# Where the context tokens stand in the loads and in the modulation of a block of gated linear attention

## The chip, the cores and the metric

The kernel runs on one core of a Trainium2 chip. The metric is the time of one execution on the device in microseconds (us). Three runs of the kernel before give a median of 1012.62 us (1012.34 to 1014.2).

The names of the engines: PE is the matrix engine (PEld its weight loads), DVE the vector engine, ACT the scalar engine, POOL the general one; SP issues most of the DMAs and computes nothing. An instruction of an engine runs when all those ahead of it on that engine have started and what it waits for is there, so one that waits holds up what stands behind it.

## What is computed

One layer of a diffusion backbone over 512 latent tokens and 256 context tokens of 1024 features, in 32-bit floats. Cut to what the change touches:

```
mod_lat = jnp.split(jax.nn.silu(c) @ w_ada + b_ada, 6, axis=-1)
mod_ctx = jnp.split(jax.nn.silu(c_ctx)[None, :] @ w_ada + b_ada, 6, axis=-1)
h_lat = modulate(rmsnorm(x, g_mix), shift, scale)      # 512 tokens
h_ctx = modulate(rmsnorm(ctx, g_mix), shift_c, scale_c)  # 256 tokens
z = h @ w_in          # q, k, v, g, dd (decay, rank 16), conv and gate columns
zd = dd @ w_dec_up + b_dec     # up-projection of the decay, 16 -> 512, two directions
log_a = log_sigmoid(zd) / 16
```

Behind that come the attention scans (the context's state is where the latent scan starts), a short convolution, the gates, an output projection, a SwiGLU layer and a last norm. They are the same before and after.

## The kernel before

Products of 32-bit precision are made of three passes: each operand is split into a high part (ACT makes it, a copy or an activation with rounding) and a low part (DVE subtracts it), and PE sums high x high, high x low and low x high. A split is thus one ACT and one DVE instruction, and PE waits for both.

The start of the kernel, some 60 us, makes the first head's q, k, v and decay columns of the latent tokens. The latent tokens (`xt`, four tiles of 128 x 1024) are loaded, normed (`normed`: ACT squares and a root, DVE a reciprocal and a product) and turned by PE into features on partitions (`turn`, the transposes `xtp`, copied out to `xsT` by ACT and DVE). Then the features are gone through in four **parts** of 256. For part p:

- `ada_load(p)` loads eight 256 KB pieces of w_ada (`wa`), `w0_load(p)` 256 rows of the needed columns of w_in in four DMAs (`r_w`, 128x2x256, 128x2x32 and twice 128x2x128 floats, 557 KB in all).
- `ada_rows(p)` multiplies `wa` on PE (`ada`), DVE copies the bank (`adar`), PE turns it to columns (`adac` in `mod_cols`), DVE makes shift and scale (`modT`, `gs`).
- `modulate(2p)` and `modulate(2p + 1)` make `h`, the modulated latent features, high part on ACT, two DVE instructions for the low one.
- `w0_split(p)` splits `r_w` (`h_w` on ACT, `l_w` on DVE), and `gather_v` and `gather_kq` add the products of k = 2p and 2p + 1 into the banks of v, k and q (`v`, `kl`, `q` on PE).

The loop over k from 0 to 7 runs one part ahead: at k = 1, 3 and 5 it splits and modulates part 1, 2 and 3. After its last part it norms the two context tiles (line 541), turns them at k = 6 (line 549) and modulates all their eight feature tiles (line 551, `mod_ctx`: `xcT` to `hc`, one ACT and two DVE instructions each). `head0_gather` then multiplies the context features (`vc`, `kc`), and ends with the transposes `ddt` of the decay's rank-16 columns, which `v_done` has put into `st`.

What sets the order: from line 481 on, the instructions of PE, ACT and DVE keep the order in which the code writes them (`keep_in_program_order`). The loads on SP don't: a planner puts a load that waits for nothing ahead of one that waits for a buffer. SP also has eight completion counters that its DMAs take in turn, so that a DMA is issued when the one eight before it has landed. Two kinds of loads wait for a buffer here: `r_w` has three buffers for four parts, so part 3's waits for the split of part 0; the context tokens take buffers of the tag `raw` that part 0's `wa` held, so they wait for PE's `ada` of part 0.

The up-projection of the decay, `wraw`, is loaded in eight copies of 16 rows by POOL at the start (line 321) and split by five DVE instructions in `wdu_split` (line 514), behind the modulation of part 0.

Of the kernel before, what the change touches and what calls it, by code (L numbers as in the profile page):

```python
# [18 lines left out]
KT = D // P  # L19
T = 512  # L20
TC = 256
NT = T // P
NC_ = TC // P
# [23 lines left out]
def hybrid_block(ctx: ExitStack, tc: tile.TileContext, x, c, ctxt, c_ctx, w_ada, b_ada, g_mix, w_in,  # L47
                 w_dec_up, b_dec, g_head, w_gla_out, w_conv, w_conv_out, w_mix_out, g_ffn,
                 w_ffn_in, w_ffn_out, g_final, out):
    nc = tc.nc  # L50
# [14 lines left out]
    def u2(name, dt=F32, shape=(P, 512)):  # L65
        return up.tile(list(shape), dt, tag="u2", name=name, bufs=NU)
# [8 lines left out]
    def uh(name, dt=F32, shape=(P, 512)):  # L75
        return up.tile(list(shape), dt, tag="uh", name=name, bufs=8)
# [29 lines left out]
    def f32(ap):  # L106
        return ap.bitcast(F32)
# [45 lines left out]
    def mm3(o, a, b, start, stop):  # L153
        mm(o, a[0], b[0], start=start, stop=False)
        mm(o, a[0], b[1], start=False, stop=False)
        mm(o, a[1], b[0], start=False, stop=stop)

    def rstd_of(ss, n, width, name):

        r = sm.tile([P, n], F32, tag=f"rs{n}", name=f"rs_{name}")  # L160
        act_.activation(r, ss, AF.Sqrt, bias=eps, scale=1.0 / width)
        dve.reciprocal(r, r)
        return r
# [4 lines left out]
    def token_load(i):  # L168
        if i < NT:
            xt = hp.tile([P, D], F32, tag="xt", name=f"xt{i}", bufs=4)  # L170
            nc.sync.dma_start(xt, x[i * P:(i + 1) * P, :])
        else:
            xt = wp.tile([P, D], F32, tag="raw", name=f"xt{i}", bufs=4)
            nc.sync.dma_start(xt, ctxt[(i - NT) * P:(i - NT + 1) * P, :])
        return xt
# [12 lines left out]
    def small_vectors(vs):  # L188
        for r0, src in vs:
            n = src.shape[1] // P  # L190
            for d in range(src.shape[0]):
                nc.sync.dma_start(vrow[r0 + d * n:r0 + (d + 1) * n, :P], src[d:d + 1, :].rearrange("o (r f) -> (o r) f", f=P))
# [52 lines left out]
    def normed(i, xt):  # L245
        junk = u2(f"junk{i}", BF16, (P, D))
        ss = sm.tile([P, 1], F32, tag="ss", name=f"ss{i}")
        act_.activation(junk, xt, AF.Square, accum_out=ss)
        dve.tensor_scalar_mul(xt, xt, rstd_of(ss, 1, D, f"x{i}"))
# [11 lines left out]
    def ada_load(p_):  # L261

        us = []
        src = w_ada[:, :2 * D].rearrange("(k p) (s f) -> p k s f", p=P, s=2)[:, :, :, p_ * 256:(p_ + 1) * 256]
        if p_ < 2:
            for k in range(0, KT, 2):
                if p_ == 0:
                    t = wp.tile([P, 2, 2, 256], F32, tag="raw", name=f"wa{p_}{k}", bufs=4)
                else:
                    t = hp.tile([P, 2, 2, 256], F32, tag="wa", name=f"wa{p_}{k}", bufs=4)  # L270
                for i in range(2):
                    nc.sync.dma_start(t[:, i], src[:, k + i])
                us += [t[:, i].rearrange("p s f -> p (s f)") for i in range(2)]
        else:
            for k in range(KT):
                t = (uh if p_ == 2 else uo)(f"wa{p_}{k}", F32, (P, 2, 256))
                nc.sync.dma_start(t, src[:, k])
                us.append(t.rearrange("p s f -> p (s f)"))
        return us

    def ada_rows(p_, us):

        rows = gbank(f"ada{p_}")
        for k in range(KT):
            g_ = 32 * (k % 4)
            mm(rows[g_:g_ + 32, :], cw[:, k, :], us[k], start=k < 4, stop=k >= KT - 4)
        rsb = u2(f"adar{p_}")
        dve.tensor_copy(rsb, rows)
        return rsb
# [5 lines left out]
    def mod_split(src, f, j, hi, lo):  # L295
        g_, sh = gs[:, f, j:j + 1], modT[:, f, 0, j:j + 1]
        act_.activation(hi, src, AF.Identity, scale=g_, bias=sh)
        dve.tensor_scalar(src, src, g_, sh, ALU.mult, ALU.add)
        dve.tensor_sub(lo, src, f32(hi))
# [13 lines left out]
    def modulate(f):  # L313
        mod_split(xsT[:, f, :], f, 0, *h[f])

    def wdu_load():
        wraw = u2("wraw")
        whi_ = u2("wdhi", F32R)
        for d in range(2):
            for r in range(4):  # L320
                nc.gpsimd.dma_start(wraw[d * 64 + r * 16:d * 64 + r * 16 + 16, :], w_dec_up[0, d])
        return wraw, whi_

    def wdu_split(wraw, whi_):
        dve.tensor_copy(whi_, wraw)
        for d in range(2):
            a = d * 64
            dve.tensor_copy(wdu[a:a + 32, :], f32(whi_)[a:a + 32, :])
            dve.tensor_sub(wdu[a + 32:a + 64, :], wraw[a + 32:a + 64, :], f32(whi_)[a + 32:a + 64, :])
# [19 lines left out]
    def run(steps):  # L349
        for _ in steps:  # L350
            pass
# [85 lines left out]
    def w0_load(p_):  # L437

        r = hp.tile([P, 2, NW + 256], F32, tag="wr", name=f"r_w0{p_}", bufs=3)
        for d0, c0, n in ((0, CV, HV), (HV, CD, 32), (NW, CK, P), (NW + P, CQ, P)):  # L440
            nc.sync.dma_start(r[:, :, d0:d0 + n], w_in[p_ * 256:(p_ + 1) * 256, c0:c0 + n].rearrange("(a p) b -> p a b", p=P))
        return r

    def w0_at(k, a, e):
        return tuple(w_[:, k % 2, a:e] for w_ in w0[k // 2])
# [12 lines left out]
    def gather(o, c0, src, k, n=T):  # L458
        mm3(o[:, :n], w0_at(k, c0, c0 + P), tuple(w_[:, :n] for w_ in src[k]), k == 0, k == KT - 1)
# [7 lines left out]

    vo = [bank(f"v0_{NC_}")]

    wdu_ = wdu_load()  # L470
    was, wrs = [], []
    for p_ in range(4):
        if p_:
            wrs.append(w0_load(p_))
        was.append(ada_load(p_))
        if p_ == 0:
            wrs.append(w0_load(p_))
    small_vectors(((R_GH, g_head), (R_BD, b_dec[0]), (R_WC, w_conv[0])))
    xcs = [token_load(NT + i) for i in range(NC_)]
    lat = (xsT[:, :4, :], xsT[:, 4:, :])  # L480
    pinned[0] = True
    normed(0, xts[0])
# [12 lines left out]
    def w0_split(p_):  # L495
        w0.append(split_raw(wrs[p_], f"w0{p_}"))

    def mod_lo(f):
        g_, sh = gs[:, f, 0:1], modT[:, f, 0, 0:1]
        src = xsT[:, f, :]  # L500
        dve.tensor_scalar(src, src, g_, sh, ALU.mult, ALU.add)
        yield
        dve.tensor_sub(h[f][1], src, f32(h[f][0]))


    w0.append(tuple(wp.tile([P, 2, NW + 256], F32R, tag=t, name=f"{t}_w00", bufs=4) for t in ("whi", "wlo")))
    act_.copy(w0[0][0], wrs[0])
    act_.activation(h[0][0], xsT[:, 0, :], AF.Identity, scale=gs[:, 0, 0:1], bias=modT[:, 0, 0, 0:1])
    lo = mod_lo(0)
    next(lo)  # L510
    dve.tensor_sub(w0[0][1], wrs[0], f32(w0[0][0]))
    run(lo)
    modulate(1)
    wdu_split(*wdu_)
    vo += [(bank if i < 3 else gbank)(f"v0_{NC_ + i}") for i in range(1, NT)]
    ko, qo = gbank("kl0"), gbank("q0")

    def mod_ctx(f):
        t = uh(f"hc{f}", F32R, (P, 2, TC))
        mod_split(xcT[f // 4][:, f % 4, :], f, 1, t[:, 0, :], t[:, 1, :])  # L520
        hc.append((t[:, 0, :], t[:, 1, :]))
# [5 lines left out]
    for k in range(KT):  # L527
        p_ = k // 2 + 1
        more = k % 2 == 1 and p_ < 4
        if more:  # L530
            w0_split(p_)
            gather_v(vo[:2], h, k)
            rsb = ada_rows(p_, was[p_])
            gather_kq(k - 1)
            mod_cols(p_, rsb)
            modulate(2 * p_)
            modulate(2 * p_ + 1)
            gather_v(vo[2:], h, k, base=2)
            if p_ == 3:
                for i in range(NC_):  # L540
                    normed(NT + i, xcs[i])
        else:
            gather_v(vo, h, k, passes=k == 0)
        if k % 2 or k >= 6:
            gather_kq(k)
        if k == 6:
            xcT = [wp.tile([P, 4, TC], F32, tag="raw", name=f"xcT{i}", bufs=4) for i in range(2)]
            for i in range(NC_):
                turn(NT + i, xcs[i], xcT, i)
            for f in range(KT):  # L550
                mod_ctx(f)
    hp.release()
    gp = tc.alloc_tile_pool(name="gp", bufs=1)
# [10 lines left out]
    def head0_gather():  # L564
        for k in range(KT + 2):
            if k < KT:
                gather_v(vc, hc, k)
            if k >= 2:
                gather(kc, NW, hc, k - 2, TC)
            if k == KT - 1:  # L570
                ddt(NC_, NC_ + NT)
                vps2 = gbank("vps2")
                tr(vps2[:, :R_N], vrow[:R_N, :P], ident[:R_N, :R_N])
                dve.tensor_copy(vec[:, 64:], vps2[:, 64:R_N])
# [370 lines left out]
    for pr in range(KT // 2):  # L945
# [24 lines left out]
        for j in range(2):  # L970
# [3 lines left out]
            hi, lo = ux(f"cuh{pr}{j}", F32R), ux(f"cul{pr}{j}", F32R)  # L974
# [20 lines left out]
    for i, t in enumerate(og):  # L995
        mk = uv if i < 3 else ux
        hi, lo = mk(f"ogh{i}", F32R), mk(f"ogl{i}", F32R)
# [3 lines left out]
    for pr in range(KT // 2):  # L1001
        ada_tick()
        sl_ = Slab(w_gla_out, pr * 256, 256, f"go{pr}")
        for j in range(2):
            i = 2 * pr + j
# [4 lines left out]
            hi, lo = ux(f"meh{i}", F32R), ux(f"mel{i}", F32R)  # L1010
# [119 lines left out]
    for pr in range(FT // 2):  # L1130
# [16 lines left out]
        for j in range(2):  # L1147
# [4 lines left out]
            hi, lo = mk(f"ah{pr}{j}", F32R), mk(f"al{pr}{j}", F32R)  # L1152
# [8 lines left out]
    for ch in range(2):  # L1161
# [9 lines left out]
        for t in range(NT):  # L1171
# [8 lines left out]
            else:  # L1180
# [4 lines left out]
                r = rstd_of(ss, 1, D, f"fin{t}")  # L1185
# [32 lines left out]
```

## Time and profile before

| | before |
|---|---|
| median of three runs | 1012.62 us |
| the profiled execution, as timed | 1013.98 us |
| its span, from first to last instruction | 1012.3 us |
| PE busy | 989.9 us (98%) |
| DVE busy | 545.7 us (54%) |
| ACT busy | 382.0 us (38%) |
| POOL busy | 6.4 us (1%) |
| data moved | 117.16 MB, mean 116 GB/s |

The start by stretches of 10 us (busy time of PE and DVE, the clock granted to PE as a share of full speed, what the DMAs moved):

| stretch, us | PE | DVE | clock | GB/s |
|---|---|---|---|---|
| 20 to 30 | 8.82 | 8.26 | 1.00 | 337 |
| 30 to 40 | 9.94 | 4.81 | 1.00 | 338 |
| 40 to 50 | 9.92 | 4.74 | 1.00 | 173 |
| 50 to 60 | 9.68 | 7.81 | 1.00 | 82 |
| 60 to 70 | 9.26 | 7.31 | 1.00 | 132 |
| 70 to 80 | 8.02 | 7.54 | 0.86 | 105 |
| 80 to 90 | 10.00 | 5.13 | 0.97 | 107 |

Busy time is read beside what the engine waited for: PE can be busy all the time and still be paced by its own order, and an engine that idles costs nothing unless another waits for it. All times below are from the start of the span of the profiled execution.

### The profile page before, as it was taken

Reading aid. Unit: us, or ns where it says so; the run is one execution under the profiler, and the core shown is the slowest. Engines: PE = TensorE matmul, PEld = TensorE weight load, DVE = VectorE, ACT = ScalarE, POOL = GpSimd, SP = SyncE. Lnnn points to the kernel's source line nnn. Section 1 sums busy time; section 2 is a strip of 40 time slices with the busy share of each in tenths; the row PEclk is TensorE's granted clock in tenths of the full one; section 3 lists DMA queues with packets and bytes.
Section 4 is the critical chain, followed back from the end, with each engine's and each line's share of the span. In section 5 each row is a group of like instructions: output and inputs, shape, how many; then the busy total and the mean of one; then the engine's idle time right before and its main releaser. Section 6 shows DMA issues by size and latency. Waiting matters only on the chain.

```text
span 1012.3 us, 12874 instructions
## 1 busy us (share of the span) xinstructions
PE 989.9 (98%) x5217; PEld 826.3 (82%) x5221; DVE 545.7 (54%) x845; ACT 382.0 (38%) x602; POOL 6.4 (1%) x18
## 2 busy tenths in 40 slices
PE   5989999999999999999999999999999999999997
PEld 3778888888788888888888888988888888888886
DVE  6577876866646677767443345643423333423424
ACT  5257464649345222224222224633322323311313
POOL 2000000000000000000000000000000000000000
PEclk9999999999999999999999999999999999999999
DMA  9841212021427776666533222242332332331302
GB/s 296 263 118 49 52 54 63 23 63 43 123 88 205 208 203 185 172 209 210 149 101 104 84 84 84 84 125 84 104 104 84 104 104 83 101 127 64 125 21 84
DMA packets 109760, 117.16 MB, mean 116 GB/s; under 512 B 5523, under 2 KB 97797, under 8 KB 109701
## 3 DMA queue, kind: packets, MB, share of 16 engines
q1 hardware_dynamic: 109444, 116.07, 38.0%
q8 instruction: 41, 0.67, 0.3%
q0 software_dynamic: 256, 0.26, 0.1%
q14 instruction: 19, 0.15, 0.1%
HBM read 114.22 MB, written 2.10 MB: 115 GB/s over the span
## 4 chain that ended last, share of the span: by engine, by line
PE 91%; DVE 4%; ACT 3%; issue 1%; DMA 1%; SPq 0%; ACTq 0%; DVEq 0%
PE f L148 24%; PE fo L148 11%; PE yc L148 4%; PE yg L148 4%; PE gb L148 4%; PE cb L148 4%; PE cc L148 4%; PE ch L148 4%; PE ga L148 4%; PE g L148 4%; PE v L148 4%; PE mx L148 3%; PE kl L148 2%; PE o L148 2%; PE q L148 2%; PE F L148 2%
## 5 line engine op out<-in xcount | busy, mean ns | idle before, releaser
L148 PE MATMUL f<-h,h_fa 128*128 128x512 f32 (+1 forms) x384 | 111.0, 372 | 0.2 <-DVE h L102 0.2
L148 PE MATMUL f<-h,h_fb 128*128 128x512 f32 (+1 forms) x384 | 110.2, 372 | 0.0
L148 PEld LDWEIGHTS f<-h,h_fa 128*128 128x128 f32 x384 | 70.2, 188 | 13.2 <-DVE h L102 0.8
L148 PEld LDWEIGHTS f<-h,h_fb 128*128 128x128 f32 x384 | 70.0, 188 | 12.4
L148 PE MATMUL f<-h,l_fb 128*128 128x512 f32 (+1 forms) x192 | 71.3, 371 | 0.0
L148 PE MATMUL f<-h,l_fa 128*128 128x512 f32 (+1 forms) x192 | 71.3, 371 | 0.0
L102 DVE TENSOR_TENSOR l_fa<-r_fa,h_fa 128x1024 fp32r<-128x1024 f32 x22 | 26.9, 1225 | 74.6 <-ACT h_fa L102 74.6
L102 DVE TENSOR_TENSOR l_fo<-r_fo,h_fo 128x1024 fp32r<-128x1024 f32 x22 | 26.9, 1224 | 68.7 <-ACT h_fo L102 68.7
L148 PE MATMUL fo<-h_fo,ah 128*128 128x512 f32 x154 | 60.5, 393 | 0.0
L148 PE MATMUL fo<-l_fo,ah 128*128 128x512 f32 x154 | 60.5, 393 | 0.0
L148 PE MATMUL fo<-h_fo,al 128*128 128x512 f32 x154 | 60.4, 392 | 0.0
L935 DVE SCALAR_TENSOR_TENSOR acc<-r_wa,c,acc 128x256 f32<-128x256 f32 x112 | 54.1, 483 | 9.1 <-DMA r_wa<-in_w_ada_dram 6.4
L102 ACT CAST h_fo<-r_fo 128x1024 fp32r<-128x1024 f32 x22 | 23.1, 1050 | 71.0 <-PE fo L148 27.4
L148 PEld LDWEIGHTS f<-h,l_fb 128*128 128x128 f32 x192 | 36.2, 188 | 6.3
L148 PEld LDWEIGHTS f<-h,l_fa 128*128 128x128 f32 x192 | 36.1, 188 | 6.3
L148 PE MATMUL g<-h,h_g 128*128 128x512 f32 x128 | 41.0, 402 | 0.0
L148 PE MATMUL gb<-h,h_gb 128*128 128x512 f32 x128 | 40.0, 394 | 0.0
L148 PE MATMUL cb<-h,h_cb 128*128 128x512 f32 x128 | 39.7, 391 | 0.0
L148 PE MATMUL ch<-h,h_ch 128*128 128x512 f32 x128 | 39.6, 390 | 0.0
L148 PE MATMUL cc<-h,h_cc 128*128 128x512 f32 x128 | 39.6, 390 | 0.0
L148 PE MATMUL ga<-h,h_ga 128*128 128x512 f32 x128 | 39.4, 390 | 0.0
L1150 DVE TENSOR_TENSOR sil<-sil,f 128x512 f32<-128x512 f32 x22 | 15.1, 687 | 39.7 <-PE f L148 39.7
(320 smaller groups left out, 2281.4 us busy)
## 6 DMA issues: line engine op xcount, KB each, us to landing
r_wa<-in_w_ada_dram SPq DMA_DIRECT2D x32, 512.0 KB
r_fa<-in_w_ffn_in_dram SPq DMA_DIRECT2D x22, 512.0 KB
r_fb<-in_w_ffn_in_dram SPq DMA_DIRECT2D x22, 512.0 KB
r_fo<-in_w_ffn_out_dram SPq DMA_DIRECT2D x22, 512.0 KB
wa<-in_w_ada_dram SPq DMA_DIRECT2D x32, 256.0 KB
r_g<-in_w_in_dram SPq DMA_DIRECT2D x8, 512.0 KB
r_gb<-in_w_in_dram SPq DMA_DIRECT2D x8, 512.0 KB
r_cc<-in_w_in_dram SPq DMA_DIRECT2D x8, 512.0 KB
```

Source lines behind the costliest of these rows:

```text
L102: return lambda *a, **k: pin(getattr(self.engine, op)(*a, **k))
L148: pe_pin(nc.tensor.matmul(*a, **k))
L935: nc.vector.scalar_tensor_tensor(acc, w_[:, k, :], ck, acc, ALU.mult, ALU.add)
L1150: nc.vector.tensor_mul(sil, sil, obs[2 + j])
```

## The change

Three things are moved, and one instruction pair is turned around. (1) In the code, the loads of the two context tiles stand behind `ada_load(1)`, ahead of part 2's loads, and no longer at the end. They are normed at k = 1, turned at k = 2, and modulated behind the latent features of the same part: feature tiles 0 to 3 at k = 3, 4 and 5 at k = 5, 6 and 7 at k = 6. (2) `wraw` is loaded on SP, behind the small vectors, instead of on POOL at the start, and split in `head0_gather` at k = 1. (3) In part 0 the low part of the weights (`wlo`) comes ahead of the features' product on DVE.

```diff
 def wdu_load():
...
-                nc.gpsimd.dma_start(wraw[d * 64 + r * 16:d * 64 + r * 16 + 16, :], w_dec_up[0, d])
+                nc.sync.dma_start(wraw[d * 64 + r * 16:d * 64 + r * 16 + 16, :], w_dec_up[0, d])
...
-    wdu_ = wdu_load()
     was, wrs = [], []
     for p_ in range(4):
...
         if p_ == 0:
             wrs.append(w0_load(p_))
+        if p_ == 1:
+            xcs = [token_load(NT + i) for i in range(NC_)]
     small_vectors(((R_GH, g_head), (R_BD, b_dec[0]), (R_WC, w_conv[0])))
-    xcs = [token_load(NT + i) for i in range(NC_)]
+    wdu_ = wdu_load()
...
     dve.tensor_scalar(src, src, g_, sh, ALU.mult, ALU.add)
-        yield
         dve.tensor_sub(h[f][1], src, f32(h[f][0]))
...
-    lo = mod_lo(0)
-    next(lo)
     dve.tensor_sub(w0[0][1], wrs[0], f32(w0[0][0]))
-    run(lo)
+    mod_lo(0)
     modulate(1)
-    wdu_split(*wdu_)
...
             gather_v(vo[2:], h, k, base=2)
-            if p_ == 3:
-                for i in range(NC_):
-                    normed(NT + i, xcs[i])
+            if p_ > 1:
+                for f in range(2 * p_ - 4 if p_ == 2 else 2 * p_ - 2, 2 * p_):
+                    mod_ctx(f)
...
-        if k == 6:
+        if k == 1:
+            for i in range(NC_):
+                normed(NT + i, xcs[i])
+        if k == 2:
             xcT = [wp.tile([P, 4, TC], F32, tag="raw", name=f"xcT{i}", bufs=4) for i in range(2)]
             for i in range(NC_):
                 turn(NT + i, xcs[i], xcT, i)
-            for f in range(KT):
+        if k == 6:
+            for f in (6, 7):
                 mod_ctx(f)
...
             if k >= 2:
                 gather(kc, NW, hc, k - 2, TC)
+            if k == 1:
+                wdu_split(*wdu_)
```

What this makes of the order on the engines. First SP before, at the end of the weights of part 2 (`wa_212` is its last piece, `r_w_214` the w_in rows of part 3, `wa_219` the first piece of part 3's w_ada):

```order
L277 DMA wa_210<-in_w_ada_dram 128x2x256
L277 DMA wa_212<-in_w_ada_dram 128x2x256
L441 DMA r_w_214<-in_w_in_dram 128x2x256
L441 DMA r_w_214<-in_w_in_dram 128x2x32
L441 DMA r_w_214<-in_w_in_dram 128x2x128 x2
L277 DMA wa_219<-in_w_ada_dram 128x2x256
```

and SP before at the end of all these loads (`wa_233` is the last piece of w_ada, `vrow` the small vectors, `xt_241` and `xt_243` the context tokens, `r_g` the first weights of the next stage):

```order
L277 DMA wa_233<-in_w_ada_dram 128x2x256
L192 DMA vrow<-in_g_head_dram 2x128
L192 DMA vrow<-in_b_dec_dram 4x128 x2
L192 DMA vrow<-in_w_conv_dram 8x128 x3
L174 DMA xt_241<-in_ctx_dram 128x1024
L174 DMA xt_243<-in_ctx_dram 128x1024
L117 DMA r_g_0_711<-in_w_in_dram 128x4x256
L117 DMA r_g_1_713<-in_w_in_dram 128x4x256
```

The same place on SP now (`wa_227` is the last piece of w_ada, `xt_183` and `xt_185` are the context tokens, `r_w_208` the w_in rows of part 3):

```order
L277 DMA wa_227<-in_w_ada_dram 128x2x256
L192 DMA vrow<-in_g_head_dram 2x128
L192 DMA vrow<-in_b_dec_dram 4x128 x2
L192 DMA vrow<-in_w_conv_dram 8x128 x3
L321 DMA wraw<-in_w_dec_up_dram 16x512 x8
L174 DMA xt_183<-in_ctx_dram 128x1024
L174 DMA xt_185<-in_ctx_dram 128x1024
L441 DMA r_w_208<-in_w_in_dram 128x2x256
L441 DMA r_w_208<-in_w_in_dram 128x2x32
L441 DMA r_w_208<-in_w_in_dram 128x2x128 x2
L117 DMA r_g_0_706<-in_w_in_dram 128x4x256
```

The context tokens stand where they stood, behind all sixteen pieces of w_ada of parts 2 and 3; `wraw` stands ahead of them, and part 3's w_in rows have gone behind them.

ACT before, from the modulation of part 1 on (`h_140` holds the features of parts 0 and 1, `h_141` those of parts 2 and 3; `h_w_448` and `h_w_512` are the weights of parts 2 and 3; `junk`, `ss` and `rs_x` belong to the context tokens' norm):

```order
L102 ACTIVATE h_140<-xsT,modT,gs 128x512 x2
L102 CAST h_w_448<-r_w_193 128x1088
L102 ACTIVATE h_141<-xsT,modT,gs 128x512 x2
L102 CAST h_w_512<-r_w_214 128x1088
L102 ACTIVATE h_141<-xsT,modT,gs 128x512 x2
L102 ACTIVATE junk_558,ss_559<-xt_241 128x1024
L102 ACTIVATE rs_x_561<-ss_559,eps 128x1
```

and ACT now from the same place (`h_w_483` and `h_w_563` are the weights of parts 2 and 3):

```order
L102 ACTIVATE h_140<-xsT,modT,gs 128x512 x2
L102 ACTIVATE junk_431,ss_432<-xt_183 128x1024
L102 ACTIVATE rs_x_434<-ss_432,eps 128x1
L102 ACTIVATE junk_438,ss_439<-xt_185 128x1024
L102 ACTIVATE rs_x_441<-ss_439,eps 128x1
L102 COPY xcT_457<-xtp_0_459 128x4x128
L102 COPY xcT_457<-xtp_0_471 128x4x128
L102 CAST h_w_483<-r_w_187 128x1088
L102 ACTIVATE h_141<-xsT,modT,gs 128x512 x2
```

The norm of the context tokens and the copies of their transposes stand ahead of everything of parts 2 and 3. On DVE it is the same, and on PE the sixteen transposes stand between the products of k = 2 and of k = 3; otherwise PE's order is as before.

## Rows read from the trace of the kernel before

**Rows 1.** Page, part 1: engine, busy us (share of the span), instructions

```profile
PE 989.9 (98%) x5217; PEld 826.3 (82%) x5221; DVE 545.7 (54%) x845; ACT 382.0 (38%) x602; POOL 6.4 (1%) x18
```

**Rows 2.** Timeline of SP's DMA issues, 30 to 46 us: start, us, instruction, count

```profile
30.60 2.53 SPq L441 DMA_DIRECT2D r_w<-in_w_in_dram  x4
33.53 5.01 SPq L277 DMA_DIRECT2D wa<-in_w_ada_dram  x8
38.59 0.32 SPq L192 DMA_DIRECT2D vrow<-in_g_head_dram  x1
...
40.67 1.79 SPq L192 DMA_DIRECT2D vrow<-in_w_conv_dram  x3
42.91 1.06 SPq L174 DMA_DIRECT2D xt<-in_ctx_dram  x2
```

**Rows 3.** Waits of SP, 38 to 46 us: us in total, times, longest

```profile
SPq L192 <- DMA wa<-in_w_ada_dram: 2.1, 5, 0.5
SPq L174 <- DMA wa<-in_w_ada_dram: 0.7, 2, 0.4
```

**Rows 4.** Windows: stretch, PE, PEld, DVE, ACT, POOL busy, clock, DMA share, GB/s

```profile
32.00:34.00 2.00, 1.94 (x12) 1.57 (x11) 1.93 (x4) 1.45 (x2) 0.00 (x0) 1.00 1.10 348
...
46.00:48.00 2.00, 2.00 (x14) 1.24 (x7) 0.69 (x1) 0.00 (x0) 0.00 (x0) 1.00 0.46 180
48.00:50.00 2.00, 2.00 (x17) 1.95 (x16) 0.33 (x2) 0.61 (x1) 0.00 (x0) 1.00 0.01 2
```

**Rows 5.** Timeline of PE: start, us, instruction, count, [idle before <- releaser]

```profile
34.41 0.43 PE L148 MATMUL v<-h_w,h 128*128 128x288 f32 x2
...
35.43 1.92 PE L148 MATMUL ada<-wa,cw 128*32 128x512 f32 x16
...
54.38 1.03 PE L151 MATMUL xtp<-ident,xt 128*128 128x128 f32 x8
...
56.61 0.38 PE L148 MATMUL v<-h_w,h 128*128 128x288 f32 x1
```

**Rows 6.** Chain of waits, 0 to 160 us: start, us, what

```profile
1.59 3.72 DMA xt<-in_x_dram
5.33 1.16 ACT junk L102 x2
```

**Rows 7.** Timeline of all engines, 0 to 14 us

```profile
7.91 3.68 PE L151 MATMUL xtp<-ident,xt 128*128 128x128 f32 x16 [4.97 <-DVE xt L102]
```

**Rows 8.** Timeline of DVE, 14 to 92 us

```profile
24.77 0.42 DVE L102 CAST wdhi<-wraw 128x512 fp32r<-128x512 f32 x1
...
27.50 1.29 DVE L102 TENSOR_TENSOR l_w<-r_w,h_w 128x1088 fp32r<-128x1088 f32 x1
...
43.39 1.28 DVE L102 TENSOR_TENSOR l_w<-r_w,h_w 128x1088 fp32r<-128x1088 f32 x1
46.72 0.69 DVE L102 COPY adar<-ada 128x512 f32<-128x512 f32 x1 [2.05 <-PE ada L148]
...
57.60 0.41 DVE L102 TENSOR_SCALAR xcT<-xcT,gs,modT 128x256 f32<-128x256 f32 x1
...
63.55 0.43 DVE L102 TENSOR_TENSOR hc<-xcT,hc 128x256 fp32r<-128x256 f32 x1
```

**Rows 9.** Timeline of PE, 14 to 92 us

```profile
48.00 0.95 PE L148 MATMUL adac<-sel,adar 128*128 128x2 f32 x8
...
69.26 0.30 PE L151 MATMUL ddt<-ident,st 128*128 128x128 f32 x1 [0.61 <-ACT st L102]
...
74.84 0.30 PE L151 MATMUL ddt<-ident,st 128*128 128x128 f32 x1 [0.92 <-ACT st L102]
75.66 0.62 PE L148 MATMUL z<-ddT,wdu 64*128 64x256 f32 x4 [0.52 <-DVE ddT L102]
```

**Rows 10.** Windows, the same columns, where the clock fell and rose

```profile
77.00:78.00 1.00, 1.00 (x4) 0.78 (x3) 0.90 (x3) 1.00 (x4) 0.00 (x0) 0.56 0.03 8
...
80.00:81.00 1.00, 1.00 (x5) 0.82 (x4) 0.27 (x1) 0.99 (x2) 0.00 (x0) 0.73 0.00 0
```

## The prediction

> **What bounds the kernel now.** The page first: PE is busy for 98% of the span [rows 1], so a change at the start pays or costs only by what it does to PE's time there. Then I read SP's issues in order of time [rows 2]. From 30 to 43 us they come in the order in which the code names them: part 3's w_in rows, part 3's eight pieces of w_ada, the small vectors, and last, at 42.91 us, the two context tokens. What paces them is not SP: each of the small vectors and of the tokens waits for a piece of w_ada to land [rows 3], eight issues back. The windows say why: while the weights come the DMAs are full, at 1.10 of their share and 348 GB/s, and after 48 us, with the tokens in, they are empty [rows 4]. This costs nothing today, since PE wants the tokens only at 54.38 us [rows 5], and between 34 and 54 us it goes from product to product without a gap worth naming.
>
> The change asks for the tokens at another time. On PE their sixteen transposes now stand between the products of k = 2 and those of k = 3. Before, that border is the second product of the row at 34.41 us, at about 34.55 us [rows 5]. So what matters is when the tokens land. In the code their load has moved ahead of part 2; on SP it has not. There it still follows the last piece of w_ada, and eight copies of `wraw` have come between. **PE will ask for the tokens at 34.5 us, and they will land at about 48.** ACT, DVE and PE keep their written order, and on all three everything of parts 2 and 3 stands behind the tokens' norm or transposes, so that nothing can run meanwhile.
>
> **When the tokens land.** (a) A small vector's issue takes 0.32 us; with the step to the next I count 0.36 for an issue that waits for nothing. Before, the second token is thus issued at 42.91 + 1.06 - 0.36 = 43.6 us, and it waits for the last piece of w_ada, which landed then [rows 2, 3]. (b) Part 3's w_in rows leave the stretch ahead of it: 557 KB at 348 GB/s are 1.6 us [rows 4]. (c) `wraw` no longer shares the DMAs at the start: 262 KB, 0.75 us; between nothing (if it slipped into gaps) and 0.75 I take the whole, since the DMAs are full. The last piece lands at 43.6 - 1.6 - 0.75 = 41.25 us. (d) By the rule of eight, the second copy of `wraw` waits for that piece, and then seven copies go ahead of the first token. If nothing holds them they cost an issue each, 0.36 us, 2.5 in all. Bounds: 0.27 each (three vectors' issues take 1.79 us with two waits in it; the least that the issues can be is about that), 1.9 us; or 0.74 each, the distance of the vectors now [rows 2], 5.2 us. I take 2.5, since what is eight back is small or landed by then. The first token is issued at 43.75 us, the second at 44.1. (e) From issue to landing the first latent token took 3.72 us [rows 6]. The second context token was issued at 43.6 and its data had ended by 48.0, when the window falls from 180 to 2 GB/s [rows 4]: 4.4 us to the last data, somewhat more to the landing; I take 4.7, between 4.4 and 5.2 (3.72, and 1.5 for the first token's 524 KB at 348 GB/s). The second token lands at 48.8 us, the first about a microsecond ahead of it.
>
> The Trainium skill ("DMA: Bandwidth & Descriptors", "Issuing engines are not separate DMA queues") says that starting DMAs on several engines saves only the issuing engine's time, which it calls usually small. By that rule moving `wraw` from POOL to SP would cost next to nothing, and the sum below would come to 1026.5 instead of 1029. I go by the issues' rows, because here eight issues stand in one queue ahead of what PE waits for.
>
> **From the landing to PE.** At the start of the kernel a latent token goes from the first square on ACT, at 5.33 us, to PE's first transpose at 7.91 us: 2.58 us for square, root, reciprocal and product [rows 6, 7]. The same for the second context token: 48.8 + 2.58 = 51.4 us. Then its eight transposes. At full clock eight take 1.03 us [rows 5]; at the start, after 4.97 us without work, sixteen took 3.68 us, 1.84 for eight [rows 7]. The half clock is granted later too: 0.56 from 77 to 78 us and 0.73 from 80 to 81, half speed from 77.1 to 80.5, after PE stood still three times within 69 to 76 us [rows 9, 10]. With some 15 us without work I take the half clock: 53.2 us, where at full clock it would be 52.4. PE resumes the products of k = 3 at 53.2 instead of 34.55 us: **18.65 us late**.
>
> **What is given back and what is added.** The transposes' old place falls away, from 54.38 to 56.61 us: -2.2 [rows 5]. A rest of half clock behind the transposes: between 0 and 1.7 (half of those 3.4 us); I take 0.4, since the gap between the two tokens' transposes counts as well. DVE: a feature tile of the context takes 0.79 us (eight from 57.60 to 63.98 [rows 8]). Four of them, 3.2 us, now stand ahead of part 3's split, which ran from 43.39 to 44.68; it would end at 47.8 and `adar` at 48.5 in old time, where PE took up `adac` at 48.00 to 48.2 [rows 8, 9]: PE waits 0.4 more. Part 3's w_in rows follow the tokens by some 2 us and are wanted 10 us after PE's resuming; they cost nothing. On ACT the same four tiles hide in its idle time.
>
> Behind k = 7 the gain that the change can have: DVE is no longer at the context's features until 63.98 us, so `v_done` and the latent `ddt` come in time, and PE's wait of 0.61 us goes [rows 9]: -0.6. The five instructions of `wdu_split`, 2.7 us (24.77 to 27.50 [rows 8]), fill most of what DVE gains there, but end before `ddt`'s copy. The waits of 0.92 and 0.52 us hang on DVE's splits behind that copy, whose distance is unchanged; I leave them, with the clock's fall at 77 us that follows. If they went too, with the clock: another -3.1. The pair that is turned around in part 0, `wdu_split`'s going from there, and the earlier loads can make PE come to the border by up to a microsecond or two sooner than 34.55. That is worth nothing: PE waits for the tokens anyway, and is late by the time at which it resumes.
>
> **Sum:** 18.65 - 2.2 + 0.4 + 0.4 - 0.6 = 16.65 us. On the profiled execution's 1013.98 us that is 1030.6; it stands 1.36 us above the median, and against the median of 1012.62 the forecast is 1029.3 us, rounded 1029.
>
> Ends: least, 1.9 us for the seven copies, 4.4 us for the landing, transposes at full clock and all the gains behind (-3.7): the second token is issued at 43.5, lands at 47.9, and PE resumes at 51.5, 16.95 late; 16.95 - 2.2 - 3.7 = +11, 1023.7. Most, no gain from `wraw`'s leaving the start (42.0), 0.74 us for each issue (the second token at 47.9), 5.2 us to land, half clock and its rest of 1.7: 53.1, resuming at 57.5, 22.95 late; 22.95 - 2.2 + 1.7 + 0.4 = +22.85, 1035.5.
>
> **The rivals.** *The tokens are there in time*, as the code reads: the loads run as written, or the DMAs serve the tokens ahead of what was issued before. The point from which it decides: both landed by 34.55 - 2.58 = 32.0 us. Then PE never waits for them. The megabyte pushes parts 2 and 3 back by 3 us, less 0.75 for `wraw`; the last piece of w_ada lands at 45.9, when PE's `ada` of part 3 is under way. What is left is +0.4 and between -0.6 and -3.7: 1009.3 to 1012.4 us. For it speaks only the source text. Against it: before, the trace's issues follow the planned order row by row [rows 2], and the 16 pieces of w_ada stand ahead in it now. 5%, three of them for faster by over 0.2% (about what a measurement of this kernel can tell from no change), two for within it.
>
> *The wait is much shorter*: SP gets through the pieces of w_ada faster without the w_in rows and POOL's copies, so that the tokens land at 38 to 46 us. That asks for over 350 GB/s where 348 is the most that these rows show. 1016 to 1023.5 us, 3%.
>
> *The wait is partly won back behind it*, since the weights of parts 2 and 3 lie ready when PE resumes. But PE had no gaps there to close: its busy time is full in the windows from 46 to 50 us [rows 4]. At most the waits counted above; this is the lower end of the forecast, no case of its own.
>
> *The tokens come later still*, if the eight copies go one landing after another: eight times 2 us or more. Over 1036 us, 3%.
>
> **How the numbers follow.** The forecast has 89%, with 1023.7 to 1035.5 us. The range 1023.5 to 1035.5 leaves out the rivals, 11%, and little of the forecast's own. Slower by over 0.2%: 0.95; within: 0.02; faster: 0.03.
>
> **What would show it.** Right: SP's issue of the context tokens at 43 to 46 us, behind all of w_ada; ACT idle from about 32.5 to 47 us until a DMA of ctx; on PE one gap from about 34 us to 50, released by DVE's `xt`, and a clock of 0.50 for some microseconds after it; PE's `xtp` of the context at 50 to 53; no wait at the latent `ddt`. Wrong: the tokens issued before 30 us; PE busy through 35 to 50 us; or a gap of that size with the time back by 160 us.

## The result, and the profile after

| | before | after |
|---|---|---|
| median | 1012.57 us (4 runs, 1012.34 to 1014.2) | 1029.91 us (4 runs, 1029.37 to 1031.88) |
| profiled execution, as timed | 1013.98 us | 1030.05 us |
| its span | 1012.3 us | 1028.3 us |
| PE busy | 989.9 us (98%) | 990.2 us (96%) |

The kernel became slower: 1.0171 times the time of before, 95% interval 1.0154 to 1.0189. PE's busy time is the same, so the 16 us of span are time in which PE stands. The runs of before fall into two groups, about 1012.5 and 1014.1 us, so that medians of before shift by some 1.1 us between the comparisons below and the ratios within one comparison are the safer numbers.

SP's issues after, in order of time (start, us, instruction, count), which answer to [rows 2]:

```profile
22.83 11.82 SPq L277 DMA_DIRECT2D wa<-in_w_ada_dram  x16
...
37.29 1.83 SPq L192 DMA_DIRECT2D vrow<-in_w_conv_dram  x3
39.47 3.78 SPq L321 DMA_DIRECT2D wraw<-in_w_dec_up_dram  x8
43.37 0.83 SPq L174 DMA_DIRECT2D xt<-in_ctx_dram  x2
44.29 2.03 SPq L441 DMA_DIRECT2D r_w<-in_w_in_dram  x4
```

The two context tokens go out at 43.37 us, behind all of w_ada and behind the eight copies of `wraw`; part 3's w_in rows follow them. The chain of waits after (start, us, what) tells what set that time, and what hung on it:

```profile
34.28 5.88 DMA wa<-in_w_ada_dram
...
40.17 0.32 SPq L321
...
42.84 0.42 SPq L321
...
43.37 3.89 DMA xt<-in_ctx_dram
...
47.34 1.16 ACT junk L102 x2
...
49.35 0.77 DVE xt L102
...
50.25 3.84 PE xtp L151 x16
```

Seven of the eight copies stand between 40.17 us, when the last piece of w_ada had landed, and 43.37 us: 3.2 us, 0.46 us each. PE's timeline after (start, us, instruction, count, idle before and its releaser) shows what PE did meanwhile; the second half answers to [rows 9]:

```profile
32.43 0.29 PE L148 MATMUL v<-h_w,h 128*128 128x288 f32 x1
50.25 3.84 PE L151 MATMUL xtp<-ident,xt 128*128 128x128 f32 x16 [17.52 <-DVE xt L102]
53.74 0.59 PE L148 MATMUL v<-h_w,h 128*128 128x288 f32 x1
...
59.76 0.38 PE L148 MATMUL v<-h_w,h 128*128 128x288 f32 x1
...
68.64 1.05 PE L148 MATMUL adac<-sel,adar 128*128 128x2 f32 x8 [0.30 <-DVE adar L102]
69.55 0.38 PE L148 MATMUL v<-h_w,h 128*128 128x288 f32 x1
...
86.60 0.60 PE L151 MATMUL ddt<-ident,st 128*128 128x128 f32 x4
...
87.86 0.63 PE L148 MATMUL g<-h,h_g 128*128 128x512 f32 x2
89.34 0.50 PE L148 MATMUL g<-h,l_g 128*128 128x512 f32 x1 [0.85 <-DVE l_g L102]
...
92.60 0.30 PE L151 MATMUL ddt<-ident,st 128*128 128x128 f32 x1 [0.92 <-ACT st L102]
93.42 0.62 PE L148 MATMUL z<-ddT,wdu 64*128 64x256 f32 x4 [0.52 <-DVE ddT L102]
...
102.97 0.28 PE L148 MATMUL v<-h_v,hc 128*128 128x256 f32 x1
```

One gap of 17.52 us, between the last product of k = 2 and the context's transposes. Windows of the same stretch (stretch; PE, PEld, DVE, ACT, POOL busy; granted clock, DMA share, GB/s), beside [rows 4]:

```profile
34.00:36.00 2.00, 0.00 (x0) 0.00 (x0) 0.00 (x0) 0.00 (x0) 0.00 (x0) 0.83 1.10 349
...
38.00:40.00 2.00, 0.00 (x0) 0.00 (x0) 0.00 (x0) 0.00 (x0) 0.00 (x0) 0.50 0.17 51
40.00:44.00 4.00, 0.00 (x0) 0.00 (x0) 0.00 (x0) 0.00 (x0) 0.00 (x0) 0.50 0.25 61
...
50.00:55.00 5.00, 4.75 (x21) 4.31 (x22) 2.59 (x6) 2.35 (x4) 0.00 (x0) 0.50 0.32 77
55.00:56.00 1.00, 1.00 (x7) 0.38 (x9) 1.00 (x1) 0.00 (x0) 0.00 (x0) 0.60 0.82 202
56.00:57.00 1.00, 1.00 (x16) 0.24 (x8) 0.07 (x1) 0.00 (x0) 0.00 (x0) 1.00 0.73 230
```

From 40 to 44 us, while SP hands out `wraw`, nothing computes and the DMAs are a quarter busy, at 61 GB/s: that stretch is bound by the issues of one queue, not by the memory. The DMAs are nearly idle even before it, at 0.17 of their share from 38 to 40 us, while SP's issues still wait one by one for the last pieces of w_ada to land, until 40.16 us; why these land so long after the data have thinned out is not shown. The clock is at its lower level (0.50, 1.2 of 2.4 GHz) until 55 us and some of the microsecond behind, so the transposes and the first products run at half speed.

### The profile page after: what moved, and what is told of

Same layout as the page of the kernel before. It is cut to its first block, busy times and chain, and to the rows that moved or that the text cites. A ratio compares the mean times of both kernels' runs of the same rounds, so it can differ in the third digit from the quotient of the medians.

```text
span 1028.3 us, 12873 instructions
## 1 busy us (share of the span) xinstructions
PE 990.2 (96%) x5221; PEld 827.2 (80%) x5221; DVE 546.2 (53%) x845; ACT 382.2 (37%) x602; POOL 2.4 (0%) x10
## 4 chain that ended last, share of the span: by engine, by line
PE 90%; DMA 3%; DVE 2%; ACT 2%; SPq 1%; issue 1%; ACTq 0%; DVEq 0%
PE f L148 23%; PE fo L148 10%; PE v L148 5%; PE yc L148 4%; PE yg L148 4%; PE gb L148 4%; PE cb L148 4%; PE ch L148 4%; PE cc L148 4%; PE ga L148 4%; PE g L148 4%; PE mx L148 3%; PE o L148 2%; PE kl L148 2%; PE q L148 2%; PE F L148 2%
## 5 line engine op out<-in xcount | busy, mean ns | idle before, releaser
L938 DVE SCALAR_TENSOR_TENSOR acc<-r_wa,c,acc 128x256 f32<-128x256 f32 x112 | 54.1, 483 | 8.0 <-DMA r_wa<-in_w_ada_dram 5.2
L148 PE MATMUL v<-h_v,h 128*128 128x256 f32 x192 | 36.3, 286 | 0.0
```

The source lines that it names most:

```text
L148: pe_pin(nc.tensor.matmul(*a, **k))
L938: nc.vector.scalar_tensor_tensor(acc, w_[:, k, :], ck, acc, ALU.mult, ALU.add)
```

## The experiments

Two questions: is it the wait for the tokens that costs the 17 us, and which of the change's three moves brings it about? The theory of the prediction says that the early use of the context is sound by itself, and that the loads' order makes it dear. The rivals: the early use costs by itself (ACT's, DVE's and PE's rows are longer ahead of parts 2 and 3), or the move of `wraw` costs what it costs whatever stands behind it.

**The up-projection back on POOL**, all else as changed. The tokens then stand on SP where the code has them, behind part 1's pieces of w_ada.

```
-                nc.sync.dma_start(wraw[d * 64 + r * 16:d * 64 + r * 16 + 16, :], w_dec_up[0, d])
+                nc.gpsimd.dma_start(wraw[d * 64 + r * 16:d * 64 + r * 16 + 16, :], w_dec_up[0, d])
...
+    wdu_ = wdu_load()
     was, wrs = [], []
...
     small_vectors(((R_GH, g_head), (R_BD, b_dec[0]), (R_WC, w_conv[0])))
-    wdu_ = wdu_load()
```

> The changed kernel with one part undone: the decay's up-projection is loaded by POOL at the start again (its split stays late). With that, the planner leaves the context tokens where the code has them, behind part 1's w_ada. Theory A, that the whole loss is PE waiting for tokens that land late: they now land near 28 us, ahead of PE's border at 33 us, the 17.5 us gap and the half clock behind it go, and what the other parts give at the start and at the latent ddt is left: 1008 to 1011 us. Rival B, that the context's norm, transposes and modulation in the middle of parts 2 and 3 are themselves what holds PE up: still over 1020 us. Rival C, that the copies on SP cost only their own issue time: 1029.9 less 3 to 4, about 1026.

Measured: 1012.89 us (11 runs), 0.9996 of before, interval 0.9987 to 1.0005. All of the loss is gone, and the gain that was expected (1008 to 1011 us) is not there. SP's issue of the tokens, in the timeline of this kernel:

```profile
22.06 0.87 SPq L174 DMA_DIRECT2D xt<-in_ctx_dram  x2
```

and PE's timeline at the context's transposes and behind:

```profile
35.15 1.06 PE L151 MATMUL xtp<-ident,xt 128*128 128x128 f32 x8 [0.56 <-DVE xt L102]
36.45 1.20 PE L151 MATMUL xtp<-ident,xt 128*128 128x128 f32 x8 [0.24 <-ACT xcT L102]
...
51.41 1.05 PE L148 MATMUL adac<-sel,adar 128*128 128x2 f32 x8 [0.30 <-DVE adar L102]
...
72.11 0.50 PE L148 MATMUL g<-h,l_g 128*128 128x512 f32 x1 [0.84 <-DVE l_g L102]
...
75.36 0.30 PE L151 MATMUL ddt<-ident,st 128*128 128x128 f32 x1 [0.93 <-ACT st L102]
```

The gap of 17.52 us has become 0.56. So neither the longer rows of ACT and DVE nor the transposes at k = 2 cost much; the rival of the early use falls. What misses is the gain: the latent `ddt` waits no more (0.61 us before), but PE waits 0.84 us for `l_g` and 0.30 us for `adar`, where before had 0.40 and nothing, and the wait of 0.92 us for the context's `st` has stayed (0.93).

**The written order forced on SP**, with `wraw` and the small vectors still ahead of the tokens. The loads of the tokens, of `wa` (two lines) and of `r_w` keep the order of the code; the diff shows two of the four.

```
-            nc.sync.dma_start(xt, ctxt[(i - NT) * P:(i - NT + 1) * P, :])
+            tc.keep_in_program_order(nc.sync.dma_start(xt, ctxt[(i - NT) * P:(i - NT + 1) * P, :]))
...
-                nc.sync.dma_start(t, src[:, k])
+                tc.keep_in_program_order(nc.sync.dma_start(t, src[:, k]))
```

> The changed kernel with the loads of w_ada, w_in and the tokens kept on SP in the order of the code, so that the tokens stand ahead of part 2's weights; the small vectors and the eight copies of the up-projection stay on SP and come ahead of the tokens. Theory A: the tokens are issued at about 29 us, behind 14 small issues, land at 33 and 34, and PE waits for them from 32.6 to about 36 us: 1012 to 1014 us. Rival B (the place of the context's work, not of its load): over 1020 us.

Measured: 1017.64 us (7 runs), 1.0036 of before, 1.0025 to 1.0047. 12.3 of the 17.3 us are gone, more is left than expected. SP's timeline in this kernel:

```profile
20.28 0.32 SPq L192 DMA_DIRECT2D vrow<-in_g_head_dram  x1
...
24.46 4.65 SPq L321 DMA_DIRECT2D wraw<-in_w_dec_up_dram  x8
29.23 0.83 SPq L174 DMA_DIRECT2D xt<-in_ctx_dram  x2
```

and PE's timeline there:

```profile
35.67 3.43 PE L151 MATMUL xtp<-ident,xt 128*128 128x128 f32 x16 [2.87 <-DVE xt L102]
...
40.07 3.67 PE L148 MATMUL ada<-wa,cw 128*32 128x512 f32 x16
```

The fourteen small copies take from 20.28 to 29.23 us on SP, and the tokens go out 7.2 us later than with `wraw` on POOL. PE waits 2.87 us for them, turns them at half clock (0.50 to 0.56 in the windows from 36 to 39 us; 3.43 us for sixteen, where the run before needed 1.06 and 1.20 for eight each at full clock), and then part 2's w_ada is late as well: `ada` takes 3.67 instead of 1.92 us [rows 5], at a clock of 1.00. So 12.3 us of the loss go with the planner's order, and 4.7 us (1017.64 - 1012.89) are left. These are not `wraw`'s alone: the six small vectors take the first 4.2 us on SP here and go out behind all of w_ada, at 41.12 us, with `wraw` on POOL; and some 1.4 us of the 4.7 come only behind `z`, where the clock falls here, to 0.62 and 0.52 in the windows from 80 to 84 us, and stays at 1.00 with `wraw` on POOL. Why the planner turns the order when `wraw` comes to SP was not looked into; that it does so is seen from the rows on SP here and with `wraw` on POOL. That loads which wait for no buffer go first does not settle it, for with `wraw` on POOL the small vectors, which wait for none, still go last.

**The context used two steps later**, loads as in the changed kernel: norm at k = 3, transposes at k = 4, feature tiles 0 to 5 modulated with part 3.

```
...
-        if k == 1:
+        if k == 3:
             for i in range(NC_):
                 normed(NT + i, xcs[i])
-        if k == 2:
+        if k == 4:
```

> The changed kernel with its loads as they are, but the context tokens normed at k = 3 and turned at k = 4 (feature tiles 0 to 5 modulated at k = 5). Theory A, PE waits from its border to a landing that doesn't move: the border comes 9.2 us of PE's work later, the wait shrinks from 17.5 to about 8 us, and the time to 1020.7 us (1019.5 to 1022). Rival B, that the loss is a cost of the work itself: about as much as now, 1028 to 1031 us.

Measured: 1020.24 us (4 runs), 1.0062 of before, 1.0048 to 1.0076. PE's timeline:

```profile
50.95 3.84 PE L151 MATMUL xtp<-ident,xt 128*128 128x128 f32 x16 [6.72 <-DVE xt L102]
```

The tokens land when they land; with part 2's products put ahead of them, PE's gap is 6.72 us instead of 17.52, and the time falls by 9.7 us. So the length of the gap is set by two things, when the tokens land and how much of PE's work stands ahead of their transposes.

**The up-projection's move alone, and half of that.** Both start from the kernel before, with the context at its old place. The first moves `wraw` to SP and its split to k = 1 of the context's products, with the low part of the weights first in part 0. The second leaves the load on POOL, where it was, and makes only the other two moves. The diff is that of the first, without the pair in part 0, which the change's diff shows.

```
-                nc.gpsimd.dma_start(wraw[d * 64 + r * 16:d * 64 + r * 16 + 16, :], w_dec_up[0, d])
+                nc.sync.dma_start(wraw[d * 64 + r * 16:d * 64 + r * 16 + 16, :], w_dec_up[0, d])
...
-    wdu_ = wdu_load()
     was, wrs = [], []
...
     xcs = [token_load(NT + i) for i in range(NC_)]
+    wdu_ = wdu_load()
...
-    wdu_split(*wdu_)
...
+            if k == 1:
+                wdu_split(*wdu_)
```

> The kernel before with the change's other parts alone: the up-projection last on SP and split late, weights' low part first in part 0; the context's norm, transposes and modulation stay where they were. The planner also sends part 3's w_in rows behind the tokens here. Theory A: these rows land near 50 us where ACT wants them at 40, PE waits at adac of part 3 from about 46 to 53 us, and the late split of the up-projection stands ahead of ddt's copy on DVE: 1017 to 1021 us. Rival: w_in rows of part 3 had slack enough, and the other parts gain at the start: 1010 to 1012 us.

> The kernel before, with the up-projection still loaded by POOL at the start, but split in the context's products behind k = 1, and with the low part of the weights first in part 0: the run with the up-projection on the load queue less that move. DVE is busy until 69.1 us there, so the 2.7 us of the split come ahead of ddT's copy and of l_g: PE's wait for l_g grows from 0.40 to about 3 us, and the gap may bring the half clock for another 1 to 2 us. 1014.8 to 1017. If so, the move of the up-projection to the load queue alone accounts for 8.5 to 10.5 us of that run's 12.3, through the wait for adar of part 3. Rival: the late split costs nothing by itself (1012.3 to 1013), and all 12.3 us are the load queue's.

Measured: 1025.34 us (4 runs), 1.0114 of before, 1.01 to 1.0127, for the first; 1016.16 us (10 runs), 1.003 of before, 1.002 to 1.004, for the second. SP's timeline of the first:

```profile
44.84 0.83 SPq L174 DMA_DIRECT2D xt<-in_ctx_dram  x2
45.76 1.94 SPq L441 DMA_DIRECT2D r_w<-in_w_in_dram  x4
```

and PE's timeline of the first:

```profile
54.73 1.87 PE L148 MATMUL adac<-sel,adar 128*128 128x2 f32 x8 [8.12 <-DVE adar L102]
```

with DVE's there:

```profile
52.79 1.29 DVE L102 TENSOR_TENSOR l_w<-r_w,h_w 128x1088 fp32r<-128x1088 f32 x1 [10.87 <-ACT h_w L102]
53.99 0.68 DVE L102 COPY adar<-ada 128x512 f32<-128x512 f32 x1
```

Here PE does not ask for the tokens early, and it still stands for 8.12 us. The planner has put part 3's w_in rows behind everything, 45.76 us instead of 30.60 [rows 2]; their split stands ahead of `adar` on DVE, and PE waits for that. The time is above the expected 1017 to 1021 us: the gap is longer than the 7 us that were told, and the clock is at 0.50 from 50 to 60 us and again from 84 to 90 us, which the expectation left out. So the rival that the move of `wraw` is dear only together with the early context falls too: the order of the loads breaks the kernel before as well, at another place. The late split is the smaller part; PE's timeline of the second kernel:

```profile
74.25 0.50 PE L148 MATMUL g<-h,l_g 128*128 128x512 f32 x1 [3.02 <-DVE l_g L102]
```

In the kernel before DVE is at the latent splits until 69.1 us, and 2.7 us of `wdu_split` ahead of `l_g` make PE's 0.40 us of waiting 3.02. Behind it the clock is at 0.50 from 76 to 82 us, longer than the 3.4 us of before. The whole is 0.3%, some 3 us; what the load queue adds is 9.2 us by the medians (1025.34 - 1016.16), 8.5 by the two ratios.

**What the early context is worth.** Two kernels with the same two moves, one on the changed kernel with `wraw` on POOL, one on the kernel before: `wdu_split` in two pieces behind the copies `adar` of parts 1 and 2, where DVE next waits for PE's `adac` (1.67 and 1.56 us with `wraw` on POOL, 1.15 and 1.57 in the kernel before), and the first two weights of the gate split inside the context's products. In the first the context's feature tiles 2 and 3 go with part 3 as well, which leaves DVE to part 3's split.

```
...
             rsb = ada_rows(p_, was[p_])
+            if p_ < 3:
+                wdu_split(*wdu_, p_ - 1)
...
+            if k in (4, 6):
+                split_unit()
...
     head0_gather()
-    split_unit()
-    split_unit()
```

> The changed kernel with the up-projection of the decay loaded by POOL at the start (as in the first of these runs), and with the vector engine's work put where it idles: the five instructions that split that up-projection stand behind the copies of parts 1 and 2 (gaps of about 1.6 us there), the splits of the first two gate weights stand inside the context's products (behind k = 4 and k = 6), and context feature tiles 2 and 3 are modulated with part 3 instead of part 2. Theory A (the early context frees DVE, but the changed kernel refilled that time with other work ahead of what PE waits for): the waits of 0.84 us for l_g, 0.92 us for the context's st and 0.30 us for adar go, the 0.52 us for ddT stays; 2 to 2.7 us below the run with POOL alone (1012.9): 1010 to 1011. Rival B (what PE waits for there is the length of the chain from its own last product, not DVE's other work): no more than 0.5 us, 1012.4 or over.

> The kernel before, context at its old place, with the same two moves: the up-projection's split behind the copies of parts 1 and 2, the splits of the first two gate weights behind k = 4 and k = 6 of the context's products. Theory A: DVE is at the context's features and the latent splits until 69.1 us, so these moves find no idle time there; the wait of 0.40 us for l_g goes, those of 0.61 and 0.92 us stay: 1012.0 to 1012.6, no difference that shows. Rival B (the early context has no part in the gain): as much gain as in the run with the early context, 1010 to 1011.

Measured: 1009.90 us (7 runs), 0.9971 of before, 0.996 to 0.9982, for the first: the fastest of all kernels here, just below the 1010 to 1011 us expected. 1014.25 us (11 runs), 1.0009 of before, 1.0001 to 1.0018, for the second: no gain. (The median of before beside these two is 1013.69 us, so that both are above the 1012.0 to 1012.6 that were told.) PE's timeline of the first:

```profile
52.14 0.95 PE L148 MATMUL adac<-sel,adar 128*128 128x2 f32 x8
...
71.69 0.39 PE L148 MATMUL g<-h,l_g 128*128 128x512 f32 x1
...
73.30 0.57 PE L151 MATMUL ddt<-ident,st 128*128 128x128 f32 x2
74.38 0.62 PE L148 MATMUL z<-ddT,wdu 64*128 64x256 f32 x4 [0.52 <-DVE ddT L102]
```

The waits for `adar`, `l_g` and `st` are gone. PE's timeline of the second, at the same rows:

```profile
71.17 0.50 PE L148 MATMUL g<-h,l_g 128*128 128x512 f32 x1 [0.31 <-DVE l_g L102]
...
73.90 0.30 PE L151 MATMUL ddt<-ident,st 128*128 128x128 f32 x1 [0.85 <-ACT st L102]
75.12 0.30 PE L151 MATMUL ddt<-ident,st 128*128 128x128 f32 x1 [0.92 <-ACT st L102]
```

With the context late, DVE has no room there, and the moves only trade one wait for another. The second kernel also lacks the turned pair of part 0, but that is not where the two part: from `adac` of part 0 to that of part 1 PE takes 10.61 us in the first and 10.33 in the second, and from there to `z` 43.75 and 46.61. So the early context can be turned into 0.3%, some 2.9 us, here with its loads in order and with the room on DVE left to what PE waits for.

## Why the prediction came out right

The place, the cause and the size were as told: 1029.91 us where 1029 was forecast, by the tokens' wait at the border of k = 2 and k = 3, with the landing behind all of w_ada and `wraw`. Followed by PE's rows, after less before, the loss builds up so:

| place on PE | later by, us | step | forecast |
|---|---|---|---|
| products of k = 3 resume (53.74, before 34.55) | 19.19 | +19.19 | +18.65 |
| `v` behind `adac` of part 2 (59.76, before 39.59) | 20.17 | +0.98, rest of half clock | +0.4 |
| `v` behind `adac` of part 3 (69.55, before 48.81) | 20.74 | +0.57, wait for `adar` | +0.4 |
| latent `ddt` (86.60, before 68.16) | 18.44 | -2.30, old place of the transposes | -2.2 |
| first `g` (87.86, before 70.55) | 17.31 | -1.13, `ddt` waits no more | -0.6 |
| `z` (93.42, before 75.66) | 17.76 | +0.45, longer wait for `l_g` | 0 |
| head 1's first `v` (102.97, before 86.82) | 16.15 | -1.61, no fall of the clock | 0 |

PE's rows of the kernel before in this table, beside those of [rows 5] and [rows 9]:

```profile
39.59 0.38 PE L148 MATMUL v<-h_w,h 128*128 128x288 f32 x1
...
48.81 0.38 PE L148 MATMUL v<-h_w,h 128*128 128x288 f32 x1
...
68.16 0.50 PE L151 MATMUL ddt<-ident,st 128*128 128x128 f32 x3
...
70.55 0.63 PE L148 MATMUL g<-h,h_g 128*128 128x512 f32 x2
...
86.82 0.28 PE L148 MATMUL v<-h_v,hc 128*128 128x256 f32 x1
```

The spans differ by 16.0 us, where 16.65 were forecast. The sum is closer than its terms: their errors go from -1.6 to +0.6 us and nearly cancel, and that is luck.

**The landing.** The last piece of w_ada landed at about 40.15 us (41.25 forecast), but each of the seven copies took 0.46 us instead of 0.36. The two misses cancel but for 0.4 us: the first token was issued at 43.37, for 43.75 forecast. It landed at 47.3 us, 3.9 later, and ACT took the second at 48.73 without a wait, so that it was there by then, as forecast (48.8). The Trainium skill ("DMA: Bandwidth & Descriptors", "Issuing engines are not separate DMA queues") calls the time of an issue "usually small relative to the DMA itself"; here the seven issues in the path take 3.2 us, beside the 3.9 us of the token behind them, and the measurement decides.

**From the landing to PE** is the step that was taken wrongly. The sum went by the second token: landing, 2.58 us, eight transposes. What binds is the first: it landed at 47.3, its product ended 2.8 us later, and then PE had sixteen transposes at half clock to do, 3.5 us, so that the second token's norm was hidden behind the first's transposes. By the forecast's own numbers that path gives 47.8 + 2.58 + 3.68 = 54.1 us, against 53.2 by the second token, and the later of the two should have been taken; measured 53.74.

**The clock.** By the windows the lower level held from about 35.3 us (0.83 in the window to 36) to about 55.8 (0.60 in the one to 56); behind the transposes that is 2 us at half speed, 0.98 us lost where 0.4 was taken (0 to 1.7 were the bounds). The price of the transposes was taken from the start of the kernel, as if the clock were at half there; but the windows of before from 8 to 12 us have 1.00, so what made those sixteen take 3.68 us is not shown to be the clock. That the sixteen behind the gap, at 0.50, took about as much (3.84 us) confirms the size and not the reading.

**The gain behind** was undersized: the wait of 0.61 us at `ddt` gave 1.13. The wait for `l_g` grew by 0.45; it had no term. On DVE `l_g` stands behind the copy of the latent `ddt`, so it starts 17.75 us later (88.06, before 70.31) where PE's first `g` comes 17.31 later. The fall of the clock at 77 us, left standing in the sum, did not come in the profiled execution after (the windows from 70 to 100 us have 1.00). That is worth 1.6 us against the profiled execution of before, which is 1.4 us above the median of before; so the medians differ by 17.34 us and the spans by 16.0.

**The rivals.** That the tokens are there in time fell with SP's row at 43.37; the run with `wraw` on POOL, which is nearest to it, gave 1012.9, half a microsecond above the 1009.3 to 1012.4 that were told. A shorter wait through faster pieces of w_ada was in part there (1.1 us earlier) and was eaten by the copies. One landing after another for the eight copies did not come.

## What to carry to other kernels

Where a planner sets the order of the loads, read its order and not the code's: one small load, moved to another queue and to the end of the loads, turned the order of loads around it, and 12.3 of the 17.3 us lost went with the written order forced. Work that is put earlier in the engines' fixed order needs its data earlier by as much, or everything behind it stands; ask first when they land. And time that is freed on an engine becomes a gain only if what the bounding engine waits for moves into it: the same two moves gave 0.3% with the early context and nothing without it.

## What the runs showed of the hardware that was not expected

- A stall of PE costs more than the idle time that its row shows. The latent `ddt` shows 0.61 us of idle before, and the products behind came 1.13 us earlier without it; `adac` of part 3 shows 0.30 us, and the products behind it came 0.57 us later. From the run with `wraw` on POOL to the fastest one, waits of 0.30, 0.84 and 0.93 us went, 2.07 together, and PE's way from the context's transposes to `z` became 2.99 us shorter (38.04 us, from 36.34 to 74.38, where it was 41.03). A part is overlap: the `ddt` start 0.10 us apart back to back (0.60 us for four, 0.50 for three) while one alone is 0.30 us long, so the one that waited started 0.80 us late and shows 0.61. Where the rest goes was not taken apart.
- Eight copies of 32 KB each left the DMAs at 0.25 of their share for 4 us, with 0.46 us for each issue; the same queue moved 349 GB/s with pieces of 256 KB from 34 to 36 us.
- A short fall of the clock behind `z` comes in some kernels and not in others. The profiled execution of before has it (0.50 from 78 to 80 us), that of the kernel after keeps 1.00 from 70 to 100 us, though PE's waits ahead are much alike: 0.61, 0.40, 0.92 and 0.52 us before, 0.85, 0.92 and 0.52 after. With `wraw` on POOL (0.84, 0.93, 0.52) it keeps 1.00 too, and with the written order forced (0.84, 0.15, 0.93, 0.52) it falls. What decides is not shown.
